# Float32 weights and tokens multiplied directly in the projections, their halves kept for the dense expert part

## The chip, the cores and the metric

The kernel runs on one core of one Trainium2 chip. The metric is the device time of one execution in microseconds (us); lower is better. In the profile the engines are PE (TensorE matmuls), PEld (TensorE's weight loads), DVE (VectorE), ACT (ScalarE), POOL (GpSimd) and SP (the queue that issues most transfers). L188 is line 188 of the kernel before.

## What is computed

Two transformer layers over 512 latent and 256 context tokens of width 1024, all in float32. Cut to what matters here:

```python
for i in range(2):
    xl = rmsnorm(hl, norm1_g[i]) * (1 + ml[1]) + ml[0]      # ml: 6 vectors from the conditioning
    xc = rmsnorm(hc, norm1_g[i]) * (1 + mc[1]) + mc[0]
    if i == 0:  # mLSTM heads and differential attention on xl @ w_in and xc @ w_in
        yl, yc = even_mixer(...)                            # each ends in concat(heads) @ w_out
    else:       # sliding-window attention, latent tokens alone
        yl = odd_mixer(...)
    hl = hl + ml[2] * yl                                    # and hc alike in layer 0
    x = rmsnorm(hl, norm2_g[i]) * (1 + ml[4]) + ml[3]
    hl = hl + ml[5] * peer(x)                               # and hc alike in layer 0
out = rmsnorm(hl, final_g)

def peer(x):   # 16384 experts of one neuron each
    q = (x @ w_q).reshape(n, 8, 2, 128)
    s = einsum('nhpd,hpkd->nhpk', q, keys)                  # scores of 2 x 128 keys per head
    # the 16 best keys of both sets, the 16 best sums of them: 128 experts a token
    gate = softmax(best sums)
    w = gate * gelu(x . u[expert])
    return sum of w * v[expert]
```

## The kernel before, in words

**Halves.** A float32 operand is split in two tiles of TensorE's rounded type float32r: the high half is the value rounded, the low half is the rest. A product of two such operands is three products of halves, high by high, high by low and low by high; a sum over 1024 rows is 8 steps of 128, so 24 matmuls of one pass each. The function `weight` (L178) loads a weight block of 512 KB, makes the high half `whi` on ACT (L185) and the low half `wlo` (L188) on DVE or POOL, in turn by the settings `WL1`, `WL2` and, in the latent mixer of layer 0, on POOL alone. `xpose` (L376) transposes a block of 128 tokens and splits it into `xth` (ACT, L383) and `xtl` (DVE, L384). `split` (L817) does the same for the mixer's output, which comes back from DRAM through a tile `yr` (L824, L825).

**Who uses them.** `projT` (L199) makes [128 outputs, T tokens] with T of 256, 384 or 512; `projN` (L208) makes [128 tokens, 256 outputs]. All projections of both mixers, both output projections and the routing's queries go through one of them. There are 195 weight blocks: 49 for the context tokens of layer 0, 67 for its latent tokens, 79 in layer 1; among them are the 18 and 27 expert blocks of the run-ahead products.

**The expert layer.** Each layer routes (`route`, L877: `scores` L858, then `select` L918), builds dense gates for 384 latent tokens (`gate_build`, L1044) and then runs over 128 groups of 128 experts (`peer`, L1323). For a group the first product `dense_u` (L1105) gives `dA`, a gelu and the gate give `dw`, and the second product (L1161) adds up in `dacc`. The first products of groups 0 to 17 (layer 0) or 0 to 26 (layer 1) run ahead, during routing and gate building. The other groups split their expert rows in `halves` (L1095) with a pool of buffers of their own.

**Gathered rows.** The context tokens and the last latent block fetch the rows of their experts one for each token by an indirect transfer that POOL issues (`gather`, L991, `uv` L998); DVE multiplies (`junkv`, L1011) or adds up (`pacc`, L1024) each row. Layer 0 has 768 such steps: 350 are issued at a low priority ahead of its dense part, 64 are left to the mixer of layer 1.

**Order.** Every engine runs its instructions in a fixed order, which the framework draws up when the program is built, by priorities and by a timeline that it simulates. [...]

**Stretches of time.** In the profiled execution: to 250 us the modulation and the context mixer of layer 0; to 420 the context tokens' routing; to 960 the latent mixer and its output projection; to 1510 routing and gate building; to 2520 the dense part; to 2955 the mixer of layer 1; to 3100 the routing's scores; to 3405 the selection and gates; then the dense part of layer 1.

The splitting of weights is this:

```python
hi = self.pw.tile(shape, F32R, name="whi", tag="whi", bufs=2)
lo = self.pw.tile(shape, F32R, name="wlo", tag="wlo", bufs=2)
nc.scalar.copy(hi, raw)
self.wcnt += 1
eng = nc.vector if self.wlo == 0 or self.wcnt % self.wlo == 0 else nc.gpsimd
eng.tensor_tensor(lo, raw, hi.bitcast(F32), op=OP.subtract)
```

## Time and profile before

| | before |
|---|---|
| three runs | 4350.32, 4350.83, 4351.87 us; median 4350.83 |
| the profiled execution's span, first to last instruction | 4350.6 us; no other time of that execution is recorded |
| busy: PE, PEld | 3739.3 us (86%), 3297.7 us (76%) |
| busy: DVE, ACT, POOL | 3715.8 us (85%), 1603.3 us (37%), 2683.4 us (62%) |
| DMA | 1093.10 MB in 16 engines, mean 251 GB/s |
| chain that ended last | PE 40%, DVE 25%, issue 15%, DMA 11%, POOL 7%, ACT 2% |

Busy times of an engine are unions over its instructions; matmuls are pipelined, so a matmul's time in a row is longer than the distance to the next one's start. The chain is followed back from the last instruction, at each step to what released it or to the instruction before it on its engine.

### The profile page before, as it was taken

The numbers are of one execution on the slowest core, as the hardware profiler recorded it, in microseconds if no ns is written. First come the engines' busy times: TensorE is split into PE (matmuls) and PEld (weight loads), VectorE is DVE, ScalarE is ACT, GpSimd is POOL, SyncE is SP. The second block draws the span as 40 slices with busy tenths as digits, with TensorE's granted clock in tenths as the row PEclk, the third lists the DMA queues.
The fourth block names the chain that finished last, engine by engine and source line by source line (L and its number), as shares of the span: only waits on it lengthen the run. The fifth ranks groups of instructions, "written<-read, shape, count | busy, mean of one in ns | idle before, by whom it ended". The sixth has DMA issues, their size and how long they took to land.

```text
span 4350.6 us, 58785 instructions
## 1 busy us (share of the span) xinstructions
PE 3739.3 (86%) x20576; PEld 3297.7 (76%) x20576; DVE 3715.8 (85%) x6089; ACT 1603.3 (37%) x2676; POOL 2683.4 (62%) x1886
## 2 busy tenths in 40 slices
PE   7977666756687699999999968899886999999999
PEld 5776654445567689988889857787875899999987
DVE  6479989979999998898989989747999887777788
ACT  4433433412115533333333325443245433333333
POOL 3146777656656677777878667112577676666664
PEclk9998888878798999999999989999989999999999
DMA  5554888788742499999899988423234987887878
GB/s 192 187 185 158 276 284 280 263 308 317 241 135 109 184 337 336 332 320 327 318 331 335 341 301 290 160 84 125 94 126 168 321 309 272 285 287 269 288 264 313
DMA packets 382487, 1093.10 MB, mean 251 GB/s; under 512 B 32671, under 2 KB 134375, under 8 KB 376046
## 3 DMA queue, kind: packets, MB, share of 16 engines
q0 software_dynamic: 147456, 536.94, 34.8%
q1 hardware_dynamic: 224942, 491.58, 32.9%
q10 hardware_dynamic: 9792, 60.82, 3.4%
q8 instruction: 162, 2.65, 0.2%
q14 instruction: 135, 1.11, 0.1%
HBM read 1020.96 MB, written 68.26 MB: 250 GB/s over the span
## 4 chain that ended last, share of the span: by engine, by line
PE 40%; DVE 25%; issue 15%; DMA 11%; POOL 7%; ACT 2%; SPq 0%; POOLq 0%; DVEq 0%; ACTq 0%
PE dacc L1161 17%; PE dA L1112 14%; POOL uv L998 4%; DVE ghot L1084 4%; DMA uv<-in_pr_u_dram,ix 3%; DMA draw<-in_uT_dram 3%; DVE junkv L1011 3%; DMA uv<-in_pr_v_dram,ix 2%; PE ops L214 1%; DVE wlo L188 1%; DVE pacc L1024 1%; PE pqps L204 1%; DVE sel L916 1%; DVE gup L1070 1%; DVE sel L913 1%
## 5 line engine op out<-in xcount | busy, mean ns | idle before, releaser
L1161 PE MATMUL dacc<-dhi,dw 128*128 128x512 f32 x3072 | 989.1, 392 | 3.4 <-ACT dw L1154 1.8
L998 POOL DMA_INDIRECT uv<-in_pr_v_dram,ix x512 | 685.6, 1339 | 405.0 <-DVE pacc L1024 297.6
L998 POOL DMA_INDIRECT uv<-in_pr_u_dram,ix x512 | 685.2, 1338 | 373.6 <-DVE pa L1011 204.3
L1011 DVE CUSTOM_DVE_ANT_0 junkv<-uv,x 128x1024 bf16<-128x1024 f32 x512 | 734.7, 1435 | 39.5 <-DMA uv<-in_pr_u_dram,ix 35.5
L1024 DVE SCALAR_TENSOR_TENSOR pacc<-uv,pw,pacc 128x1024 f32<-128x1024 f32 x508 | 705.1, 1388 | 26.9 <-DMA uv<-in_pr_v_dram,ix 23.0
L1161 PEld LDWEIGHTS dacc<-dhi,dw 128*128 128x128 f32 x3072 | 579.9, 189 | 120.7 <-ACT dw L1154 2.1
L1101 ACT CAST dhi<-draw 128x1024 fp32r<-128x1024 f32 x467 | 489.2, 1050 | 463.6 <-DMA draw<-in_uT_dram 165.9
L1161 PE MATMUL dacc<-dlo,dw 128*128 128x512 f32 x1536 | 604.4, 394 | 11.1 <-DVE dlo L1102 11.0
L1102 POOL TENSOR_TENSOR dlo<-draw,dhi 128x1024 fp32r<-128x1024 f32 x210 | 545.5, 2598 | 95.6 <-ACT dhi L1101 91.9
L188 POOL TENSOR_TENSOR wlo<-wraw,whi 128x1024 fp32r<-128x1024 f32 x111 | 280.0, 2523 | 426.0 <-ACT whi L185 282.1
L1151 DVE TENSOR_TENSOR dz<-dz,dG 128x384 f32<-128x384 f32 x256 | 402.4, 1585 | 89.9 <-ACT dz L1121 88.5
L1154 ACT CAST dw<-dz 128x384 fp32r<-128x384 f32 x256 | 131.4, 513 | 690.8 <-PE dacc L1161 669.8
L1102 DVE TENSOR_TENSOR dlo<-draw,dhi 128x1024 fp32r<-128x1024 f32 x257 | 336.1, 1308 | 27.3 <-ACT dhi L1101 18.1
L185 ACT CAST whi<-wraw 128x1024 fp32r<-128x1024 f32 x195 | 204.3, 1049 | 416.6 <-PE pqps L204 101.5
L1112 PE MATMUL dA<-xth,dhi 128*128 128x384 f32 x1688 | 334.8, 340 | 10.1 <-ACT dhi L1101 6.9
L1161 PEld LDWEIGHTS dacc<-dlo,dw 128*128 128x128 f32 x1536 | 289.8, 189 | 70.1 <-DVE dlo L1102 13.3
L1112 PE MATMUL dA<-xtl,dhi 128*128 128x384 f32 x1688 | 327.4, 335 | 0.0
L1112 PEld LDWEIGHTS dA<-xth,dhi 128*128 128x128 f32 x1688 | 305.1, 189 | 28.5 <-ACT dhi L1101 7.8
L1112 PE MATMUL dA<-xth,dlo 128*128 128x384 f32 x1688 | 326.7, 334 | 0.0
L1090 PE MATMUL gps<-ghot 128*128 128x128 f32 x1536 | 231.8, 307 | 104.5 <-DVE ghot L1084 80.2
L1090 PEld LDWEIGHTS gps<-ghot 128*128 128x128 f32 x1536 | 211.2, 216 | 126.3 <-issue 84.4
L1112 PEld LDWEIGHTS dA<-xtl,dhi 128*128 128x128 f32 x1688 | 296.7, 188 | 0.0
(379 smaller groups left out, 6836.6 us busy)
## 6 DMA issues: line engine op xcount, KB each, us to landing
draw<-in_pr_v_dram SPq DMA_DIRECT2D x256, 512.0 KB
draw<-in_uT_dram SPq DMA_DIRECT2D x211, 512.0 KB
wraw<-in_wb_dram SPq DMA_DIRECT2D x150, 512.0 KB
gd<-gch ACTq DMA_DIRECT2D x48, 1024.0 KB
dG<-gd SPq DMA_DIRECT2D x30, 1536.0 KB
wraw<-in_mod_t_dram SPq DMA_DIRECT2D x48, 512.0 KB
wraw<-in_uT_dram SPq DMA_DIRECT2D x45, 512.0 KB
wraw<-in_mod_w_dram SPq DMA_DIRECT2D x32, 512.0 KB
```

The lines of the kernel that those rows point to most:

```text
L185: nc.scalar.copy(hi, raw)
L188: eng.tensor_tensor(lo, raw, hi.bitcast(F32), op=OP.subtract)
L998: nc.gpsimd.indirect_dma_start(out=t, out_offset=None, in_=a[table], in_offset=bass.IndirectOffsetOnAxis(ap=ix[:, c:c + 1], axis=0))
L1011: nc.vector.tensor_tensor_reduce(out=junk, in0=u, in1=x, op0=OP.mult, op1=OP.add, scale=1.0, scalar=0.0, accum_out=A[:, c:c + 1])
L1024: nc.vector.scalar_tensor_tensor(acc, v, W[:, c:c + 1], acc, op0=OP.mult, op1=OP.add)
L1084: eng.tensor_tensor(h.rearrange("p t (a b) -> p t a b", b=16), up[:, e, t0:t0 + 4, :].unsqueeze(3).broadcast_to([128, 4, 8, 16]), low[:, e ...
L1090: nc.tensor.matmul(ps[:, t0 - 8 * q + t, :], hot[0][:, t, :], hot[1][:, t, :], start=True, stop=True)
L1101: nc.scalar.copy(hi, raw)
L1102: eng.tensor_tensor(lo, raw, hi.bitcast(F32), op=OP.subtract)
L1112: nc.tensor.matmul(A, u[ui][:, k, :], xt[xi][:, k, 0:ND], start=(i == 0), stop=(i == 23))
L1151: nc.vector.tensor_tensor(z3, z3, self.G[:, :, j % JG, :], op=OP.mult)
L1161: self.nc.tensor.matmul(acc[b][:, h, :], w[wi][:, 128 * b:128 * b + 128], v[vi][:, 512 * h:512 * h + 512], start=(j == 0 and i == 0), stop ...
```

## The change

`weight` returns the loaded float32 tile itself, with 5 buffers in place of 3 raw, 2 high and 2 low. `projT` and `projN` issue 8 float32 matmuls in place of 24 of halves. `xpose` copies the transposed tokens once, into one float32 tile. The mixer's output (`mixed`, before `split`) is loaded straight into that tile. The run-ahead products in `dense_u` take the float32 operands. Ahead of the dense part, `peer` splits the 384 tokens into `xh` (8 ACT copies and 8 DVE subtractions of 128x384); the dense part itself keeps its halves. The second buffer of the dense gates takes the place of the token tile. The loads of the first modulation use the new tiles. Changed lines, without those where a comment alone is removed and without the ones that follow from a name:

```diff
     def weight(self, src, shape):
-        nc = self.nc
-        raw = self.pw.tile(shape, F32, name="wraw", tag="wraw", bufs=3)
-        nc.sync.dma_start(raw, src)
-        hi = self.pw.tile(shape, F32R, name="whi", tag="whi", bufs=2)
-        lo = self.pw.tile(shape, F32R, name="wlo", tag="wlo", bufs=2)
-        nc.scalar.copy(hi, raw)
-        self.wcnt += 1
-        eng = nc.vector if self.wlo == 0 or self.wcnt % self.wlo == 0 else nc.gpsimd
-        eng.tensor_tensor(lo, raw, hi.bitcast(F32), op=OP.subtract)
-        return hi, lo
+        raw = self.pw.tile(shape, F32, name="wraw", tag="wraw", bufs=5)
+        self.nc.sync.dma_start(raw, src)
+        return raw
     def projT(self, ps, w, x, T, c0=0):
-        i = 0
-        for wi, xi in ((0, 0), (0, 1), (1, 0)):
-            for k in range(8):
-                self.nc.tensor.matmul(ps, w[wi][:, k, :], x[xi][:, k, c0:c0 + T],
-                                      start=(i == 0), stop=(i == 23))
-                i += 1
+        for k in range(8):
+            self.nc.tensor.matmul(ps, w[:, k, :], x[:, k, c0:c0 + T], start=(k == 0), stop=(k == 7))
     def projN(self, ps, w2, x, b):
...
+        for k in range(8):
+            self.nc.tensor.matmul(ps, x[:, k, 128 * b:128 * b + 128], w2[k // 4][:, k % 4, :],
+                                  start=(k == 0), stop=(k == 7))
     def mod_first(self):
...
-                if n < 8:
+                if n < 7:
                     if n % 4 == 0:
-                        four = self.xt.tile([128, 4, D], F32, name="fraw", tag="xt" + "hl"[n // 4])
+                        four = self.xt.tile([128, 4 - n // 4, D], F32, name="fraw", tag=("xt", "xhh")[n // 4])
                     raw = four[:, n % 4, :]
                 else:
-                    pool, tag, bufs = (self.pg, "uv", 5) if n < 13 else (self.pw, "wraw", 3)
+                    pool, tag, bufs = (self.pg, "uv", 5) if n < 12 else (self.pw, "wraw", 5)
     def xpose(self, x, xt, b):
...
-        hi = xt[0][:, :, 128 * b:128 * b + 128]
-        nc.scalar.copy(hi, p)
-        nc.vector.tensor_tensor(xt[1][:, :, 128 * b:128 * b + 128], p, hi.bitcast(F32), op=OP.subtract)
+        nc.scalar.copy(xt[:, :, 128 * b:128 * b + 128], p)
     def xt_tiles(self, T):
-        return tuple(self.px.tile([128, 8, T], F32R, name="xt" + x, tag="xt" + x) for x in "hl")
+        return self.px.tile([128, 8, T], F32, name="xt", tag="xt")
-    def split(self, l, bb, T):
+    def mixed(self, l, bb, T):
...
-            y = self.wk.tile([128, 2, T], F32, name="yr", tag="xn", bufs=2)
-            nc.sync.dma_start(y, self.yd[l, 128 * k:128 * k + 256, 128 * bb:128 * bb + T]
+            nc.sync.dma_start(xt[:, k:k + 2, :], self.yd[l, 128 * k:128 * k + 256, 128 * bb:128 * bb + T]
                               .rearrange("(k p) t -> p k t", p=128))
-            nc.scalar.copy(xt[0][:, k:k + 2, :], y)
-            nc.vector.tensor_tensor(xt[1][:, k:k + 2, :], y, xt[0][:, k:k + 2, :].bitcast(F32), op=OP.subtract)
     def dense_u(self, j, u, A, xt):
...
+        if j < self.upre:
+            self.projT(A, u, xt, ND)
+        else:
+            i = 0
+            for ui, xi in ((0, 0), (0, 1), (1, 0)):
...
     def load_gates(self, j, blocks):
...
-            self.G = self.dn.tile([128, ND // 16, JG, 16], F32, name="dG", tag="dG%d" % (j // JG % 2), bufs=1)
+            pool, tag = ((self.dn, "dG"), (self.xt, "xt"))[j // JG % 2]
+            self.G = pool.tile([128, ND // 16, JG, 16], F32, name="dG", tag=tag, bufs=1)
     def peer(self, l, xt, bb, gat, rows, done, late, put):
...
             gat += [(bb + b, LAT, sel[b]) for b in range(nd, nb)]
+            xh = [self.xt.tile([128, 8, ND], F32R, name="xh" + x, tag="xh" + x) for x in "hl"]
+            for k in range(8):
+                nc.scalar.copy(xh[0][:, k, :], xt[:, k, 0:ND])
+                nc.vector.tensor_tensor(xh[1][:, k, :], xt[:, k, 0:ND], xh[0][:, k, :].bitcast(F32), op=OP.subtract)
+            xt = xh
```

## Rows read from the trace of the kernel before

**Rows 1.** Windows by stretch: engines' busy us (instructions), granted clock, DMA share, GB/s

```profile
core 0: us, PE busy (x) PEld busy (x) DVE busy (x) ACT busy (x) POOL busy (x), PEclk, DMA share, GB/s
0.00:250.00 250.00, 208.95 (x1441) 162.93 (x1442) 130.75 (x249) 111.51 (x288) 63.48 (x59) 0.94 0.55 192
250.00:960.00 710.00, 482.97 (x2677) 405.48 (x2677) 629.57 (x1201) 245.14 (x611) 478.44 (x371) 0.83 0.74 251
960.00:1510.00 550.00, 393.06 (x2197) 343.38 (x2195) 531.93 (x1400) 165.35 (x169) 347.07 (x290) 0.86 0.56 200
1510.00:2520.00 1010.00, 991.22 (x4917) 892.27 (x4917) 923.02 (x899) 362.97 (x486) 767.85 (x455) 0.99 0.93 329
2520.00:2955.00 435.00, 361.44 (x2661) 319.80 (x2660) 320.45 (x381) 190.20 (x466) 169.23 (x157) 0.94 0.57 201
2955.00:3100.00 145.00, 133.12 (x668) 114.17 (x667) 126.65 (x646) 41.73 (x55) 44.42 (x39) 0.95 0.33 115
3100.00:3405.00 305.00, 233.26 (x1372) 217.68 (x1372) 286.22 (x557) 144.77 (x139) 210.82 (x169) 0.90 0.41 150
```

**Rows 2.** The chain that ended last, 250 to 960 and 960 to 1510, shares by line

```profile
by line: issue 18.7%; DMA uv<-in_pr_u_dram,ix 11.0%; DMA uv<-in_pr_v_dram,ix 6.4%; DVE pacc L1024 5.3%; POOL uv L998 4.6%; DVE junkv L1011 4.1%; DMA yr<-yd 2.8%; PE dao L797 2.5%; PE vps L214 2.1%; DMA mr<-modd 2.1%; PE ops L214 1.9%; DVE w
...
by line: issue 20.5%; DVE ghot L1084 14.0%; DVE junkv L1011 8.5%; DMA uv<-in_pr_u_dram,ix 5.2%; DVE gup L1070 4.6%; DVE sel L916 4.1%; DVE wlo L188 3.8%; DVE sel L913 3.8%; DVE glow L1070 3.5%; DVE sel L912 3.0%; DVE s L914 2.9%; DVE sel L9
```

**Rows 3.** Windows of line L188 alone (low halves of weights), by stretch

```profile
core 0: us, DVE busy (x) POOL busy (x), PEclk, DMA share, GB/s
0.00:250.00 250.00, 23.54 (x17) 43.58 (x18) 0.94 0.55 192
250.00:960.00 710.00, 14.25 (x9) 85.38 (x34) 0.83 0.74 251
960.00:1510.00 550.00, 32.10 (x19) 48.30 (x19) 0.86 0.56 200
2520.00:2955.00 435.00, 24.83 (x18) 46.00 (x18) 0.94 0.57 201
2955.00:3100.00 145.00, 14.60 (x10) 27.84 (x11) 0.95 0.33 115
3100.00:3405.00 305.00, 18.09 (x11) 28.93 (x11) 0.90 0.41 150
```

**Rows 4.** Low halves of tokens, from L384's own view: min/median/max ns

```profile
L384 DVE TENSOR_TENSOR xtl<-xps,xth x26: 1198/1220/1226, 47.9 to 2967.2; 128x1024 fp32r<-128x1024 f32 x26
```

**Rows 5.** Timelines of DVE and POOL near 1050 us: start us, us

```profile
1047.28 1.20 DVE L1011 CUSTOM_DVE_ANT_0 junkv<-uv,x 128x1024 bf16<-128x1024 f32 x1
...
1049.34 3.89 DVE L1011 CUSTOM_DVE_ANT_0 junkv<-uv,x 128x1024 bf16<-128x1024 f32 x1
...
1049.72 2.42 POOL L188 TENSOR_TENSOR wlo<-wraw,whi 128x1024 fp32r<-128x1024 f32 x1
```

**Rows 6.** Row products on DVE, 250 to 960, then 960 to 1510: count | busy us, mean ns

```profile
L1011 DVE CUSTOM_DVE_ANT_0 junkv<-uv,x 128x1024 bf16<-128x1024 f32 x129 | 181.7, 1409 | 27.8 <-DMA uv<-in_pr_u_dram,ix 25.9
...
L1011 DVE CUSTOM_DVE_ANT_0 junkv<-uv,x 128x1024 bf16<-128x1024 f32 x93 | 130.9, 1407 | 7.9 <-DMA uv<-in_pr_u_dram,ix 7.5
```

**Rows 7.** Timelines of POOL and DVE in layer 1's scores

```profile
2988.74 2.39 POOL L188 TENSOR_TENSOR wlo<-wraw,whi 128x1024 fp32r<-128x1024 f32 x1 [8.45 <-PE pqps L204]
...
2989.38 0.29 DVE L912 MAX8 sel<-pss 128x8 f32<-128x128 f32 x1
```

**Rows 8.** Chain pieces of 24 matmuls of halves, 512 and 384 columns: start us, us

```profile
3000.83 5.46 PE pqps L204 x24
...
3405.46 4.19 PE dA L1112 x24
```

**Rows 9.** Timeline of PE: halves at 256 columns, then float32 at 512 and 256

```profile
2930.25 0.63 PE L214 MATMUL ops<-whi,xth 128*128 128x256 f32 x4
2930.72 0.63 PE L214 MATMUL ops<-wlo,xth 128*128 128x256 f32 x4
...
867.61 0.60 PE L772 MATMUL das<-kdc,qpd 128*128 128x256 f32 x2
868.04 1.02 PE L772 MATMUL das<-ktd,qpd 128*128 128x512 f32 x2
868.90 0.60 PE L772 MATMUL das<-kdc,qpd 128*128 128x256 f32 x2
```

**Rows 10.** The page's row of the high halves of weights

```profile
L185 ACT CAST whi<-wraw 128x1024 fp32r<-128x1024 f32 x195 | 204.3, 1049 | 416.6 <-PE pqps L204 101.5
```

More of the change, by code (lines that the diff above doesn't have):

```diff
@@ L114, in __init__ @@
         self.wk = None
-        self.wcnt, self.wlo, self.ghot = 0, WL1, 0
+        self.ghot = 0
         nc = self.nc
@@ L199, in projT @@
     def projT(self, ps, w, x, T, c0=0):
-        i = 0
-        for wi, xi in ((0, 0), (0, 1), (1, 0)):
-            for k in range(8):
-                self.nc.tensor.matmul(ps, w[wi][:, k, :], x[xi][:, k, c0:c0 + T],
-                                      start=(i == 0), stop=(i == 23))
-                i += 1
-    def projN(self, ps, w2, x, b):
-        i = 0
-        for half in range(2):
-            for xi, wi in ((0, 0), (0, 1), (1, 0)):
-                for k in range(4):
-                    self.nc.tensor.matmul(
-                        ps, x[xi][:, 4 * half + k, 128 * b:128 * b + 128], w2[half][wi][:, k, :],
-                        start=(i == 0), stop=(i == 23))
-                    i += 1
+        for k in range(8):
+            self.nc.tensor.matmul(ps, w[:, k, :], x[:, k, c0:c0 + T], start=(k == 0), stop=(k == 7))
+    def projN(self, ps, w2, x, b):
+        for k in range(8):
+            self.nc.tensor.matmul(ps, x[:, k, 128 * b:128 * b + 128], w2[k // 4][:, k % 4, :],
+                                  start=(k == 0), stop=(k == 7))
     def mod_prep(self):
@@ L241, in mod @@
                 for h in range(2):
-                    raw = self.pw.tile([128, 8, 128], F32, name="wraw", tag="wraw", bufs=3)
+                    raw = self.pw.tile([128, 8, 128], F32, name="wraw", tag="wraw", bufs=5)
                     nc.sync.dma_start(raw, a["mod_t"][l, m, 2 * q + h])
@@ L321, in mod_rows @@
             for k in range(8):
-                raw = self.pw.tile([128, D], F32, name="wraw", tag="wraw", bufs=3)
+                raw = self.pw.tile([128, D], F32, name="wraw", tag="wraw", bufs=5)
                 nc.sync.dma_start(raw, a["mod_w"][l][128 * k:128 * k + 128, m * D:m * D + D])
@@ L698, in head_out @@
         else:
-            hi, lo = (t[:, k, tok] for t in self.yx)
-            nc.scalar.copy(hi, pt)
-            nc.vector.tensor_tensor(lo, pt, hi.bitcast(F32), op=OP.subtract)
+            nc.scalar.copy(self.yx[:, k, tok], pt)
     def rope(self, ps, T, outs, c0=0, scale=None):
@@ L830, in out_proj @@
         nc = self.nc
-        xt = xt or self.split(l, hb, 128 * nb)
+        xt = self.mixed(l, hb, 128 * nb) if xt is None else xt
         m2 = self.modrow(l, s, 2)
@@ L1108, in dense_u @@
         nc = self.nc
-        i = 0
-        for ui, xi in ((0, 0), (0, 1), (1, 0)):
-            for k in range(8):
-                nc.tensor.matmul(A, u[ui][:, k, :], xt[xi][:, k, 0:ND], start=(i == 0), stop=(i == 23))
-                i += 1
+        if j < self.upre:
[4 more added lines that the diff above has]
+                for k in range(8):
+                    nc.tensor.matmul(A, u[ui][:, k, :], xt[xi][:, k, 0:ND], start=(i == 0), stop=(i == 23))
+                    i += 1
         if j % (self.ahead + 1) <= self.upre:
@@ L1345, in peer @@
             gat += [(bb + b, LAT, sel[b]) for b in range(nd, nb)]
+            xh = [self.xt.tile([128, 8, ND], F32R, name="xh" + x, tag="xh" + x) for x in "hl"]
+            for k in range(8):
+                nc.scalar.copy(xh[0][:, k, :], xt[:, k, 0:ND])
+                nc.vector.tensor_tensor(xh[1][:, k, :], xt[:, k, 0:ND], xh[0][:, k, :].bitcast(F32), op=OP.subtract)
+            xt = xh
             left, done = 256 * len(gat) - done - late, 0
@@ L1402, in run @@
                     self.mod(0, M1)
-                    self.yx = [self.px.tile([128, 8, 256], F32R, name="yx" + x) for x in "hl"]
+                    self.yx = self.px.tile([128, 8, 256], F32, name="yx")
                     self.even(CTX, xt, 2, 0)
@@ L1408, in run @@
                                            lambda: self.mod(0, F5[0]), self.yx)
-                    self.px, self.wlo = px, WL2
+                    self.px = px
                     with self.phase("rt"):
@@ L1420, in run @@
                         next(rows)
-                self.px, self.wlo = px, 1 << 30
+                self.px = px
                 self.even(LAT, xt, 4, 2)
-                self.wlo = 2
             with self.phase("op"):
```

1 line of the change is left out of this document (removed).

## The prediction

> **What bounds the kernel now.** I read the windows by stretch first, because TensorE's 86% over the whole span hides stretches with different limits. Both dense parts are TensorE's: between 1510 and 2520 us it is busy 991 of 1010 us [rows 1], and neither the change's matmuls nor its splits of weights lie there. What can move is the other 2395 us. There the reader should put PE and DVE side by side. From 250 to 1510 us DVE is busy 629.57 + 531.93 = 1161.5 of 1260 us (92%; 97% from 960 on) and PE 876.0 (70%). From 3100 to 3405 it is 94% against 76%. From 2955 to 3100, the scores of layer 1, PE leads with 92%, and in the first stretch and the mixer of layer 1 it leads too, with 84% and 83% against 52% and 74% [rows 1].
>
> The chain of waits, read second, says how far a busy engine sets the end. From 960 to 1510 the named pieces are mostly DVE's: one-hot rows, row products, searches. From 250 to 960 DVE has a smaller part; 11.0% and 6.4% are waits for gathered rows on their way, and 18.7% is issue [rows 2]. So DVE time removed after 960 should come back nearly in full, before 960 in part.
>
> **What the change takes off.** Off ACT go 195 high halves of 1.05 us, 204 us in all [rows 10]; ACT is busy for 29% to 47% of the stretches, so I cost this at nothing [rows 1]. If ACT were on the path, the same 204 us would be the price. Off DVE and POOL go the low halves: 127 us on DVE and 280 us on POOL over the six stretches [rows 3]. Off DVE also go the tokens' low halves at 1.22 us [rows 4], 26 from transposes and 4 in the load of the mixer's output, which has the same 1024 columns.
>
> POOL's 280 us matter for a second reason. A row product on DVE takes 1.20 us, but 3.89 us when a POOL low half of 2.42 us runs inside it: DVE lost 2.69 us [rows 5]. The 222 row products between 250 and 1510 average 1.41 us, so they alone lost 222 x 0.21 = 46 us [rows 6] beside 133.7 us of POOL low halves [rows 3]. Other two-operand instructions must lose too, so the stall that goes lies between 46 and 134 us in that stretch. I take 0.6 of POOL's time, 80 us, above the lower end because the 46 covers one kind of instruction. Not every DVE instruction loses: a search for the maximum, which reads one operand, takes 0.29 us while a POOL low half is running [rows 7]. In layer 1's scores, where DVE has little else, I therefore count no stall. [...]
>
> **What it adds.** A group of 24 matmuls of halves takes 5.46 us at 512 columns and 4.19 at 384 [rows 8]; at 256 columns 4 take 0.47 us (2930.25 to 2930.72), so 24 take 2.82 [rows 9]. A float32 matmul stands in the trace as two records. One record at 512 columns takes (868.90 - 868.04)/2 = 0.43 us, at 256 columns (868.04 - 867.61)/2 = 0.215 [rows 9]. Sixteen records are then 6.88 us at 512, 3.44 at 256, and between them about 5.16 at 384, which no row shows directly. A group grows by 1.42, 0.97 and 0.62 us. The code has 45 groups at 512 columns, 47 at 384 and 131 at 256: 64 + 46 + 81 = 191 us more PE work. [...]
>
> **The sum by stretch.** PE's extra counts by a quarter where DVE leads, because PE then has 24 to 32% idle to take it, by a half where PE leads among waits on other engines, and in full where matmuls run back to back.
>
> - To 250: 33 groups at 256, +20.5 us, half: +10. Removed DVE work is off the path there; I take 4 us of it for shorter starts. Net +6.
> - 250 to 960: off DVE 14.3 us of weights [rows 3], ten token or output halves (12.2 us) and 0.6 x 85.4 = 51 us of stalls, 78 in all. Half of it, since the chain holds row transfers and issue: -39. PE: 56 groups at 256 and 13 at 512, +53 us, a quarter: +13. Net -26.
> - 960 to 1510: off DVE 32.1 + 4.9 + 0.6 x 48.3 = 66 us. The new split of tokens puts back 8 instructions of at most 0.6 us (half of [rows 4]), 5 us; 61 remain. Three quarters: -46. PE: 16 groups at 512 and 18 at 384, +40 us, a quarter: +10. Net -36.
> - 2520 to 2955: 42 groups at 256 and 2 at 384, +28 us, half: +14. DVE sheds 24.8 us, some ten token halves and 28 us of stalls, but it doesn't lead: -6. Net +8.
> - 2955 to 3100: the 16 score groups run back to back, and 5.46 us each [rows 8] become 6.88: +23. Four token halves ahead of them go: -3. Net +20.
> - 3100 to 3405: off DVE 18.1 + 0.6 x 28.9 - 5 = 30 us, three quarters: -23. PE: 27 groups at 384, +26 us, a quarter: +7. Net -16.
> - Dense parts: 0. They keep their buffers and halves, and the split of tokens is counted above. The second gate buffer waits for the token tile's last reader, which is that split, some groups before group 8 needs the buffer; if that cover were gone, one load of 1.5 MB would stand open per layer, 6 us at the mean of 251 GB/s.
>
> Together 6 - 26 - 36 + 8 + 20 - 16 = -44 us. From the profiled span of 4350.6 us this is 4307 us; the span lies 0.2 us from the runs' median of 4350.83, so nothing is added.
>
> The 2 raw buffers more replace the 2 prepared blocks of before, so loads run as far ahead: I cost this at nothing, because the DMA share outside the dense parts is 0.33 to 0.74 [rows 1] (uncovered, a 512 KB block would cost 2.1 us at the mean of 251 GB/s). Gathered steps keep their number; since POOL issues them in order behind its low halves, they can start up to 2.4 us earlier behind each of 53.
>
> **The rivals.**
>
> *TensorE takes over (slower).* The added passes land on the path in proportion to PE's busy share: 0.84 x 20.5 + 0.68 x 53 + 0.71 x 40 + 0.83 x 28 + 23 + 0.76 x 26 = 17 + 36 + 28 + 23 + 23 + 20 = 147 us. Against this stand the same gains as in my sum, 4 + 39 + 46 + 6 + 3 + 23 = 121. The result is +26, 4377, and a few us more where a single projection heads a chain of waits: up to 4390. It decides once more than 63% (121/191) of the added work lies on the path; my sum has 10 + 13 + 10 + 14 + 23 + 7 = 77 us there (40%). For it: 83 to 92% busy in three of the six stretches. Against: from 250 to 1510 PE is idle 384 us.
>
> *DVE's time comes back in full.* All 78 + 61 + 30 us in place of 39 + 46 + 23: another -61, 4246; with stalls at their upper end, POOL's whole 133.7 us in place of 80, up to 50 more, 4196. For it: 97% and 94% busy. Against: the waits for rows and issue in the chain.
>
> *No change.* Between 250 and 960 DVE only waits longer for gathered rows (17.4% of the chain already), and the 39 us don't come: 4346. For it: a DMA share of 0.74 there. Against: DVE is busy for 89% of that stretch, waiting little.
>
> **How the numbers follow.** A measurement of this kernel can tell about 0.2% (9 us) from no change. Chances: my sum, 4260 to 4340, 0.48; full return, 0.17; no change, 0.11; TensorE takes over, 0.24. Faster is 0.48 + 0.17 = 0.65, same 0.11, slower 0.24. The range of 8 in 10 goes from 4205, near the lower end of full return, to 4390, the end of the slower case. The likeliest time is 4307.
>
> **What would show it.** PE busy should rise by about 190 us and DVE fall by 200 to 300 (127 of weights, 37 of tokens, the stalls). Row products between 250 and the dense part should average near 1.2 us in place of 1.41. Score groups in layer 1 should repeat 1.4 us later each. A run-ahead group at 384 columns should take 5.1 to 5.2 us. The first dense part should begin some 55 us sooner, the mixer of layer 1 should be longer by 8, and from its end to the second dense part nothing should change by more than 10. I am wrong if the row products stay above 1.35 us, for then something else on POOL stalls them; if PE in 250 to 1510 passes 80% busy with DVE waiting for projections; or if the built order places the gathered rows elsewhere, so that mixer and routing shift against one another.

## The result and the profile after

The changed kernel takes 4249.89 us (median of four runs, 4238.75 to 4256.38) against 4351.35 (4350.32 to 4356.29) for the kernel before: the ratio is 0.9761, 95% interval 0.9745 to 0.9777. 101 us were gained where 44 were forecast. The profiled execution took 4256.38 us with a span of 4254.5; it lies 96 us below the profiled span of before.

The page of the changed kernel gives the engines' busy time and the chain by engine:

```profile
PE 3836.0 (90%) x18792; PEld 3131.2 (74%) x18792; DVE 3429.5 (81%) x5975; ACT 1416.7 (33%) x2493; POOL 2376.5 (56%) x1775
...
PE 49%; DVE 18%; DMA 13%; issue 11%; POOL 7%; ACT 2%; SPq 0%; POOLq 0%; ACTq 0%; DVEq 0%
```

DVE fell by 286 us and POOL by 307; PE rose by 97 only, not by 190. The chain went from 25% DVE to 18% and from 40% PE to 49%.

To compare stretches I use events in place of fixed times, since everything shifts. First starts in the two traces, us:

| event | before | after | shift | gained in the stretch that ends here |
|---|---|---|---|---|
| context queries (`pqps`) | 254.5 | 260.9 | +6.4 | +6.4 |
| latent queries, layer 0 | 1024.4 | 1006.0 | -18.4 | -24.8 |
| `dacc`, layer 0 | 1525.1 | 1442.4 | -82.7 | -64.3 |
| queries of layer 1 | 2968.6 | 2871.5 | -97.1 | -14.4 |
| end of the last query, layer 1 | 3072.9 | 2996.4 | -76.5 | +20.6 |
| `dacc`, layer 1 | 3393.8 | 3296.3 | -97.5 | -21.0 |

The forecast's steps were +6, -26, -36, +8, +20, -16. Four are within 5 us. The two that miss are the scores, selection and gates of layer 0 (28 us more gained) and the stretch with the mixer of layer 1 (22 more); the border at 960 lies in the output projection, so the first of these is a little blurred.

Windows of the kernel before, from the latent mixer to its output projection, then the scores of layer 0, then those of the changed kernel: the same two, the selection, and the scores of layer 1 [rows 1 have the columns].

```profile
345.60:907.70 562.10, 373.20 (x1862) 305.03 (x1862) 506.11 (x796) 206.53 (x550) 410.02 (x322) 0.81 0.77 258
1024.40:1200.50 176.10, 127.75 (x480) 101.31 (x480) 172.00 (x594) 24.51 (x31) 105.39 (x97) 0.79 0.77 262
```

```profile
349.80:922.90 573.10, 400.43 (x1591) 285.65 (x1591) 487.90 (x758) 180.28 (x522) 384.24 (x313) 0.82 0.81 284
...
1006.00:1138.10 132.10, 125.56 (x354) 61.66 (x355) 124.11 (x568) 8.49 (x16) 61.56 (x72) 0.96 0.75 271
1138.10:1222.70 84.60, 74.17 (x415) 48.73 (x413) 83.69 (x402) 5.63 (x15) 36.54 (x46) 0.97 0.46 150
...
2871.50:2996.40 124.90, 124.90 (x369) 62.30 (x370) 87.28 (x558) 9.43 (x18) 16.74 (x27) 0.98 0.27 93
```

The latent mixer became 11 us longer; the scores of layer 0 became 44 us shorter. In the scores DVE was busy for 172.00 of 176.1 us and is now for 124.11 of 132.1: the bound has become PE, 95% busy. In the scores of layer 1 PE has no idle time left.

Row products on DVE (count | busy us, mean ns), in the kernel before ahead of the latent queries (345.6 to 1024.4 us), from there to the end of selection (none follows until the dense part), and over 250 to 1510; then the same of the changed kernel (349.8 to 1006; to the gates' end; 250 to 1427):

```profile
L1011 DVE CUSTOM_DVE_ANT_0 junkv<-uv,x 128x1024 bf16<-128x1024 f32 x157 | 219.3, 1397 | 32.4 <-DMA uv<-in_pr_u_dram,ix 30.3
...
L1011 DVE CUSTOM_DVE_ANT_0 junkv<-uv,x 128x1024 bf16<-128x1024 f32 x66 | 94.5, 1432 | 5.6 <-DMA uv<-in_pr_u_dram,ix 5.5
...
L1011 DVE CUSTOM_DVE_ANT_0 junkv<-uv,x 128x1024 bf16<-128x1024 f32 x222 | 312.6, 1408 | 35.7 <-DMA uv<-in_pr_u_dram,ix 33.5
```

```profile
L987 DVE CUSTOM_DVE_ANT_0 junkv<-uv,x 128x1024 bf16<-128x1024 f32 x177 | 223.2, 1261 | 57.1 <-DMA uv<-in_pr_u_dram,ix 55.0
...
L987 DVE CUSTOM_DVE_ANT_0 junkv<-uv,x 128x1024 bf16<-128x1024 f32 x46 | 55.6, 1208 | 7.0 <-DMA uv<-in_pr_u_dram,ix 6.8
...
L987 DVE CUSTOM_DVE_ANT_0 junkv<-uv,x 128x1024 bf16<-128x1024 f32 x222 | 277.6, 1250 | 64.0 <-DMA uv<-in_pr_u_dram,ix 61.8
```

The 222 products are the same, at 1.25 us in place of 1.41. But 20 of them went from behind the latent queries to ahead of them: 177 in place of 157, and 46 in place of 66. So time that DVE gained in the latent mixer shows up later, as rows that no longer take DVE's time in the scores.

The chain of the changed kernel has the new groups at their full size, 16 records at 512 columns and at 384:

```profile
2888.62 6.87 PE pqps L194 x16
...
3121.64 5.16 PE dA L194 x16
```

These are the 6.88 and 5.16 us of the forecast. The price of a group was right at this clock (0.98 granted in the scores of layer 1, 0.95 in its gates).

### The profile page after: what moved, and what is told of

It reads as the page before. It is cut to its first block, busy times and chain, and to the rows that moved or that the text cites. A ratio compares the mean times of both kernels' runs of the same rounds, so it can differ in the third digit from the quotient of the medians.

```text
span 4254.5 us, 54646 instructions
## 1 busy us (share of the span) xinstructions
PE 3836.0 (90%) x18792; PEld 3131.2 (74%) x18792; DVE 3429.5 (81%) x5975; ACT 1416.7 (33%) x2493; POOL 2376.5 (56%) x1775
## 4 chain that ended last, share of the span: by engine, by line
PE 49%; DVE 18%; DMA 13%; issue 11%; POOL 7%; ACT 2%; SPq 0%; POOLq 0%; ACTq 0%; DVEq 0%
PE dacc L1141 17%; PE dA L1091 13%; POOL uv L974 5%; DMA uv<-in_pr_v_dram,ix 4%; DMA uv<-in_pr_u_dram,ix 3%; DMA draw<-in_uT_dram 3%; PE ops L199 3%; PE dA L194 3%; PE pqps L194 2%; DVE junkv L987 2%; PE gps L1066 2%; DVE ghot L1060 2%; POOL dlo L1078 1%; PE oo L1298 1%; DVE sel L941 1%
## 5 line engine op out<-in xcount | busy, mean ns | idle before, releaser
L987 DVE CUSTOM_DVE_ANT_0 junkv<-uv,x 128x1024 bf16<-128x1024 f32 x512 | 700.1, 1367 | 69.2 <-DMA uv<-in_pr_u_dram,ix 65.1
L1077 ACT CAST dhi<-draw 128x1024 fp32r<-128x1024 f32 x467 | 489.5, 1050 | 494.4 <-DMA draw<-in_uT_dram 162.5
L1091 PE MATMUL dA<-xhh,dhi 128*128 128x384 f32 x1688 | 334.5, 340 | 11.3 <-ACT dhi L1077 6.9
L1091 PE MATMUL dA<-xhl,dhi 128*128 128x384 f32 x1688 | 327.6, 335 | 0.0
L1091 PE MATMUL dA<-xhh,dlo 128*128 128x384 f32 x1688 | 326.7, 334 | 0.3 <-POOL dlo L1078 0.3
L1091 PEld LDWEIGHTS dA<-xhh,dhi 128*128 128x128 f32 x1688 | 305.0, 189 | 29.4 <-ACT dhi L1077 7.3
L194 PE MATMUL pqps<-xt,wraw 128*128 128x512 f32 (+1 forms) x768 | 289.9, 532 | 8.8 <-DMA wraw<-in_wb_dram 6.2
L1091 PEld LDWEIGHTS dA<-xhl,dhi 128*128 128x128 f32 x1688 | 296.9, 188 | 0.1
L1091 PEld LDWEIGHTS dA<-xhh,dlo 128*128 128x128 f32 x1688 | 295.6, 188 | 0.7 <-POOL dlo L1078 0.6
L1135 DVE TENSOR_TENSOR dw<-dz,dw 128x384 fp32r<-128x384 f32 x256 | 170.4, 666 | 150.5 <-ACT dw L1134 150.5
L1066 PE MATMUL gps<-ghot 128*128 128x128 f32 x1536 | 219.2, 301 | 75.8 <-DVE ghot L1060 59.7
```

The costliest lines, as they stand in the source:

```text
L194: self.nc.tensor.matmul(ps, w[:, k, :], x[:, k, c0:c0 + T], start=(k == 0), stop=(k == 7))
L987: nc.vector.tensor_tensor_reduce(out=junk, in0=u, in1=x, op0=OP.mult, op1=OP.add, scale=1.0, scalar=0.0, accum_out=A[:, c:c + 1])
L1066: nc.tensor.matmul(ps[:, t0 - 8 * q + t, :], hot[0][:, t, :], hot[1][:, t, :], start=True, stop=True)
L1091: nc.tensor.matmul(A, u[ui][:, k, :], xt[xi][:, k, 0:ND], start=(i == 0), stop=(i == 23))
L1135: i = nc.vector.tensor_tensor(wl, z, wh.bitcast(F32), op=OP.subtract)
```

## The experiments

Each was timed in three rounds beside the kernel before, whose medians there were 4348.5 to 4352.6. Medians:

| label | kernel | us |
|---|---|---|
| | changed | 4249.89 |
| e8, e7 | changed, 4 or 3 raw buffers | 4261.41, 4258.69 |
| e2 | changed, 4 raw buffers, POOL's subtractions of weights back | 4335.37 |
| e3 | changed, 4 raw buffers, DVE's back | 4293.79 |
| e9, e17 | changed, 4 or 3 raw buffers, both back | 4385.21, 4388.71 |
| e18 | e17, tokens' halves and staged load back | 4406.22 |
| e11 | changed, 4 raw buffers, tokens' halves back | 4270.32 |
| e10 | changed, 3 raw buffers, weights copied by ACT | 4264.17 |
| e5 | changed, staged load | 4250.15 |
| e4 | changed, 6 of 8 matmuls a group | 4143.38 |
| e14 | before, 30 matmuls a group | 4418.88 |
| e1 | before, low halves all on DVE | 4297.14 |
| e15 | before, routing on DVE | 4300.63 |
| e16 | e1, routing on DVE | 4247.62 |
| e6, e12 | changed, one-hot rows on DVE; gates' product too | 4230.48, 4237.72 |
| e13 | e12, selection's products on DVE too | 4186.45 |

Runs of one kernel spread by 5 to 28 us, so a difference of less than about 10 us between two medians is not held to be one.

**Subtractions put back, POOL's alone, DVE's alone, neither.** The products stay float32; `raw - raw` goes to a tile that nothing reads, in the turn of before. POOL's alone:

```diff
     def weight(self, src, shape):
...
-        raw = self.pw.tile(shape, F32, name="wraw", tag="wraw", bufs=5)
+        raw = self.pw.tile(shape, F32, name="wraw", tag="wraw", bufs=4)
         self.nc.sync.dma_start(raw, src)
+        self.wcnt += 1
+        if self.wlo == 0 or self.wcnt % self.wlo == 0:
+            pass
+        else:
+            lo = self.pw.tile(shape, F32R, name="wlo", tag="wlo", bufs=1)
+            self.nc.gpsimd.tensor_tensor(lo, raw, raw, op=OP.subtract)
         return raw
```

> The changed kernel, with POOL's 111 low-half subtractions put back in the turn of before; their results are used by nothing, the products stay float32, and the raw tiles have 4 buffers in place of 5 to make room. Theory A (the gain is mainly POOL's: its low halves stalled DVE's two-operand instructions and stood before the gathers): with stalls of 0.6 of POOL's time, back in full in the three stretches where DVE leads (51 + 29 + 17 us), about 4250 + 97 = 4347 us, and the row products between 250 us and the first dense part average 1.4 us again. By the shares of the prediction (half, three quarters, three quarters) 26 + 22 + 13 = 61: 4311. Theory B (the gain is DVE's own instructions that went): under 4265, whatever the row products take.

> The changed kernel, with DVE's 84 low-half subtractions of weights put back in the turn of before; their results are used by nothing, and the raw tiles have 4 buffers in place of 5. No POOL subtraction stands beside them, so each should take the 1.22 us of a token's low half. Theory B (DVE's own work): the 39 in the three stretches where DVE leads come back in full, 48 us, and some of the others: 4298 to 4310. By the shares of the prediction (half of 11, three quarters of 23 and of 13) 33: 4283. Theory A (POOL's stalls are the gain): under 4270, since DVE now has slack before it leads again.

> The changed kernel with 4 raw buffers in place of 5 and nothing else: what the two runs with subtractions put back are to be held against. The prediction costed the depth at nothing: 4250, within 9 us. The rival is that loads which run further ahead are a part of the gain that the sum left out: 4265 or more, with longer waits of PE for weights at the start of projections.

Against the 4261 with 4 buffers POOL's 111 subtractions cost 74 us, more than by the prediction's shares (61), less than in full (97). DVE's 84 cost 32, as the shares say. Neither theory holds alone: B wanted under 4265 with POOL's back, A under 4270 with DVE's. The timelines of DVE and of POOL in the run with POOL's show how:

```profile
1042.92 1.23 DVE L993 CUSTOM_DVE_ANT_0 junkv<-uv,x 128x1024 bf16<-128x1024 f32 x1
...
1044.20 2.78 DVE L993 CUSTOM_DVE_ANT_0 junkv<-uv,x 128x1024 bf16<-128x1024 f32 x1
...
1047.02 1.22 DVE L993 CUSTOM_DVE_ANT_0 junkv<-uv,x 128x1024 bf16<-128x1024 f32 x1
...
1048.29 2.79 DVE L993 CUSTOM_DVE_ANT_0 junkv<-uv,x 128x1024 bf16<-128x1024 f32 x1
```

```profile
1043.70 2.20 POOL L186 TENSOR_TENSOR wlo<-wraw 128x1024 fp32r<-128x1024 f32 x1
...
1047.83 2.16 POOL L186 TENSOR_TENSOR wlo<-wraw 128x1024 fp32r<-128x1024 f32 x1
```

Each subtraction that starts at 1043.70 and 1047.83 ends at 1045.90 and 1049.99; the row product that starts behind it (1044.20, 1048.29) ends 1.08 us and 1.09 us after that end, as though it had only then begun. Where POOL starts first, as in these two pairs, the row product takes 2.78 and 2.79 us. The row products just before, at 1042.92 and 1047.02, started 0.78 and 0.81 us ahead of POOL; they took their usual 1.2 us, and POOL's took 2.20 and 2.16 us where most of POOL's that meet no row product take 1.90.

**Low halves on DVE, in the kernel before** (`WL1, WL2 = 1, 1`, and the latent mixer's too):

> The kernel before with all low halves of weights on DVE: no POOL subtraction of a weight is left outside the dense parts, and DVE has 111 more of 1.22 us, 135 us in all, 78 of them where DVE leads. Theory A with stalls in full: 4351 - 97 + 78 = 4332. By the prediction's shares 4351 - 61 + 48 = 4338. Theory B (stalls cost little): 4351 + 60 = 4410.

It gained 51 us on the 4348.54 timed beside it, though DVE has 111 instructions more; that is more than either form of theory A had expected. Row products fell to 1.27 us. POOL's halves were a loss already in the kernel before.

**Both put back.**

> The changed kernel with all 195 unused subtractions put back, on POOL and DVE in the turn of before, 4 raw buffers. If POOL's and DVE's shares add (74 and 32 over the 4261 of the run with 4 buffers): 4367. If they draw on one slack: 4340. What is left of the difference to the kernel before is then float32 on TensorE, the high halves and the tokens' halves together: the prediction's sum puts these at +77 and about -17, 4411; a time near 4350 means that the added passes cost about as little as the tokens' halves gave.

124 over the run with 4 buffers, 18 more than 74 + 32. The two wrote one scratch tile; with a tile each and 3 buffers:

> The changed kernel with 3 raw buffers in place of 5: what the next two are held against. With 4 buffers it was 4261 (11 us more). If depth has its price on each step, 4272; if only the block that is loaded ahead counted, 4261.

> The changed kernel with 3 raw buffers and all 195 unused subtractions, DVE's and POOL's results in a tile of their own each; in the run before they shared one tile, so that DVE had to wait for POOL's. If the 18 us by which both together cost more than each alone (124 against 74 + 32) came from that shared tile: 106 over the run with 3 buffers alone. If from DVE and POOL stalling one another: 124 again.

4389 against 4259 is 130, so the shared tile wasn't it: with both put back the row products average 1.40 us, as before the change, against 1.36 with POOL's alone. DVE's 84 now cost some 56 us on top of POOL's 74, where alone they cost 32. That each makes the other dearer was measured twice (18 and 24 us); by which waits was not looked into. The buffers beyond 3 or 4 are worth 9 to 11 us, near what the spread lets one tell; the prediction had them at nothing.

**Tokens, copies, staged load.** Each by itself, from the changed kernel:

```diff
+        hi = self.pw.tile(shape, F32, name="whi", tag="whi", bufs=2)     # e10, in weight
+        self.nc.scalar.copy(hi, raw)
+        return hi
...
+        lo = self.pw.tile([128, 8, 128], F32R, name="xlo", tag="xlo", bufs=1)   # e11, in xpose
+        nc.vector.tensor_tensor(lo, p, xt[:, :, 128 * b:128 * b + 128], op=OP.subtract)
...
+            y = self.wk.tile([128, 2, T], F32, name="yr", tag="xn", bufs=2)     # e5, in mixed
+            nc.sync.dma_start(y, self.yd[l, 128 * k:128 * k + 256, 128 * bb:128 * bb + T]
...
+            nc.scalar.copy(xt[:, k:k + 2, :], y)
```

> The changed kernel with each weight block copied by ACT to a second float32 tile, from which the products read it, as the high half was made before: 3 raw buffers and 2 copies, 195 copies of about 1.05 us, 204 us on ACT. The prediction costed these at nothing: 4250, within 9, or 4261 with the run of 4 buffers as a measure of loads that run less far ahead. Theory D (what the sum left out is the step between a weight's arrival and its product, and ACT's time): 58 us of the measured gain are in no run yet (101 us gained, 81 us of it lost again to TensorE by the run with six of eight matmuls, so 182 in all, of which the subtractions of weights are 124); with all of the 58 here 4308, with half 4279.

> The changed kernel with the 26 low halves of transposed tokens put back on DVE, their results unused, 4 raw buffers: 26 x 1.22 = 32 us. By the prediction's shares about 19 us over the 4261 with 4 buffers: 4280. Theory D (the 58 us that are left lie with the weights' copies): under 4275. Theory E (they lie with the tokens, which stand at the head of every projection): 4300 or more.

> The changed kernel with the mixer's output loaded through two staging tiles and copied by ACT, as before, without a low half. The prediction costed the direct load at its low halves alone: 4250 within 9. Theory C (the wait for these copies ahead of both output projections is a part of the gain that the sum left out: in the kernel before PE waited 31 us for them): 4270 to 4280, with the output projection of the latent mixer begun later.

None costs much: 5 us for 195 copies of 1.05 us on ACT against the 3-buffer run, 9 for the tokens against the 4-buffer run, nothing for the staged load by the medians (in its profile the first `dacc` comes 7 us later, at 1449.7, and a dense part that is 13 us shorter makes up for it). Theories C, D and E fall as larger causes. The staged load did delay PE at the output projection, and the first query came 19 us later (1024.7 in place of 1006.0); the gates of layer 0 then began at 1226.9 in place of 1222.7, as DVE, not PE, leads to the end of that stretch (83.69 of 84.60 us in the changed kernel). PE's row of that run and of the changed kernel, 880 to 1030 us:

```profile
L199 PE MATMUL ops<-wraw,xt 128*128 128x256 f32 x256 | 62.1, 405 | 31.7 <-ACT xt L803 28.5 <-DVE ot L822 3.2
```

```profile
L199 PE MATMUL ops<-wraw,xt 128*128 128x256 f32 x232 | 53.8, 396 | 16.2 <-DMA xt<-yd 11.9 <-DVE ot L820 4.3
```

All of it together, on top of both subtractions:

> The same, with the 26 low halves of transposed tokens and the staged load of the mixer's output (its ACT copy and its low half on DVE) put back as well, their results unused. Everything that DVE and POOL did before is then done again, and float32 on TensorE, ACT's copies of weights and the waits for halves are what is left of the change. If the tokens' halves cost the 9 us of the run that had them alone: 9 over the run before it. If they cost more where DVE has no slack, which would close the 17 us that no run has found: 25 to 35 over it, near the 4419 of the kernel before with 30 matmuls a group.

17.5 us over the run before it, twice the 9 that the tokens cost by themselves, less than the 25 expected for closing the gap. What remains against the kernel before (4406 - 4352 = 54 us) is float32 on TensorE and the new split of the tokens, less ACT's copies and the waits for halves.

**TensorE's added work by itself.** From the changed kernel with `range(6)` for `range(8)` in `projT` and 6 of 8 steps in `projN`, which leaves a quarter of each sum out, and from the kernel before with 6 more matmuls, low half by low half:

```diff
+        for k in range(6):
+            self.nc.tensor.matmul(ps, w[1][:, k, :], x[1][:, k, c0:c0 + T], start=False, stop=(i == 29))
+            i += 1
```

> The changed kernel with 6 of the 8 matmuls in each group of a projection and of a run-ahead product; a quarter of each sum is left out. A group at 512 columns takes 12 records of 0.43 us, 5.16 us, near the 5.46 of halves before, so this takes off TensorE about what the change put on, 45 x 1.72 + 47 x 1.29 + 131 x 0.86 = 251 us against the 191 added. By the prediction's share of 40% on the path 251 x 0.4 = 100: 4250 - 100 = 4150. If the added passes are hidden but in the scores of layer 1: 4250 - 16 x 1.72 = 4222. If TensorE became the bound of the projections everywhere, 63% or more, 4092 or less.

> The kernel before, halves and all, with 30 matmuls in place of 24 in each group of a projection and of a run-ahead product: the 6 more are low half by low half. A group takes 5.46 x 30 / 24 = 6.83 us at 512 columns (float32: 6.88), 5.24 at 384 and 3.53 at 256; 62 + 49 + 93 = 204 us are added, near the 191 of the change, and nothing else moves. By the prediction's share of 40%: 4351 + 82 = 4433. By what the other runs leave (the run with all subtractions put back lies 35 us above before and still lacks the tokens' halves, 9, and the weights' copies, up to 14): 4351 + 58 = 4409 or less. If DVE's lead covers nearly all of it in the kernel before: 4351 + 23 for the scores of layer 1 and little more, under 4385.

The first gained 107 of 251 us (43%), near the forecast's 40%; the second cost 67 of 204 (33%). For the 191 of the change that is 81 by the kernel whose DVE is relieved and 63 by the one whose DVE is loaded; the 54 of the run above is near the second. Busy windows of the queries alone in layer 0, then layer 1, of the kernel before, and of the changed one, show where 16 of the rest stayed:

```profile
1024.40:1200.50 176.10, 108.93 (x384) 84.16 (x384) 8.20 (x14) 0.79 0.77 262
2968.60:3073.00 104.40, 92.33 (x384) 72.20 (x384) 8.78 (x15) 0.98 0.28 94
```

```profile
1006.00:1138.10 132.10, 115.08 (x256) 49.08 (x256) 8.07 (x14) 0.96 0.75 271
2871.50:2996.40 124.90, 114.68 (x256) 48.34 (x256) 8.76 (x15) 0.98 0.27 93
```

(The columns are PE, PEld, ACT, granted clock, DMA share, GB/s.) At equal clocks, in layer 1, the queries grew by 22.4 us, as forecast. In layer 0 they grew by 6.2, because halves ran there at a mean granted clock of 0.79, with PE busy for 73% of the stretch, and float32 at 0.96, with PE busy for 95%. The same 384 matmuls of halves took 108.93 us at 0.79 and 92.33 at 0.98. The 0.79 is a mean over the stretch: from 1007 to 1030 us the granted clock was 0.50, from 1031 to 1081 it was 1.00.

**Where POOL still does two-operand work.** `GENG = "v"` puts all one-hot rows on DVE; the next runs also move the gates' product and the selection's products:

```diff
-GENG = "vpvpvvvp"
+GENG = "v"
...
-            nc.gpsimd.tensor_tensor(ge, ge, diff.unsqueeze(2).broadcast_to([128, 4, 16, 16]), op=OP.mult)
+            nc.vector.tensor_tensor(ge, ge, diff.unsqueeze(2).broadcast_to([128, 4, 16, 16]), op=OP.mult)
...
-                nc.gpsimd.tensor_tensor(low[:, 1], low[:, 1],
+                nc.vector.tensor_tensor(low[:, 1], low[:, 1],
```

> The changed kernel with all one-hot rows of the gate building on DVE (before: 120 of 192 a layer there, 72 on POOL). In the first gate building DVE's 120 average 1.07 us beside POOL's, their median is 0.69. Theory A carried further (POOL instructions with two operands slow DVE's): 192 x 0.69 = 132 us in place of 122, no stalls in the others, and PE no longer waits for POOL's rows: 4250 - 10 to - 30. The rival: DVE leads in the gate building and any added instruction there is paid: 144 x 0.69 = 99 us less 92 of stalls, 4255 or more.

> The run with all one-hot rows on DVE (4230), and the gates' multiplication into the low rows (22 of 1.0 us a layer on POOL) on DVE too. Theory A, that POOL's two-operand work costs DVE more than its own doing: 22 x 0.5 us on DVE a layer against stalls of the same size, 4220 to 4230. The rival, that DVE's added time is paid in full: 4252.

> The same, and the multiplications of the selection (128x1024, 2.5 us on POOL) on DVE too, 1.23 us each: no two-operand instruction of POOL is then left in the routing. Selection is where DVE leads with 84 of 85 us. Theory A: each took DVE about 0.5 us of stall and a wait of its own for POOL's 2.5 us, so within 10 us of the run before it, either way. The rival: DVE's time is paid in full, 32 x 1.23 = 39 us more, 4260 or above.

The one-hot rows gained 19 us, as theory A said. The gates' product alone moved nothing that can be told. With the selection's products on DVE as well, 4186.45 us: 63 under the changed kernel, 51 under the run before it, where theory A had expected no change and the rival a loss. It is the best of all (0.9624 of the kernel before, 0.9608 to 0.964). One-hot rows on DVE in the changed kernel, and in this one, first layer:

```profile
L1060 DVE TENSOR_TENSOR ghot<-gup,glow 128x512 f32<-128x512 f32 x120 | 122.1, 1069 | 14.9 <-PE gps L1066 14.9
```

```profile
L1060 DVE TENSOR_TENSOR ghot<-gup,glow 128x512 f32<-128x512 f32 x192 | 119.4, 677 | 3.8 <-PE gps L1066 3.6
...
L944 DVE TENSOR_TENSOR sel<-sel 128x1024 f32<-128x1024 f32 x16 | 19.4, 1211 | 0.0
```

DVE makes 192 in less time than it made 120 beside POOL's 72. Of the selection's 40 products the 16 for the latent tokens of layer 0 are shown; they take 1.21 us each on DVE, and the step no longer crosses to POOL and back. Which of the two, POOL's relief or the crossing that is saved, gives the 51 us isn't shown.

**Does the gain need float32 products?** The same relief of POOL on the kernel before, and on the kernel with all low halves on DVE:

> The kernel before with the one-hot rows, the gates' multiplication and the selection's multiplications on DVE; the low halves of weights stay on POOL and DVE in turn. The changed kernel gained 64 us from the same edit (4250 to 4186). If that edit and the change work apart from one another: 4351 - 64 = 4287. If the low halves on POOL still stall DVE's added instructions as well: a third to a half of it, 4320 to 4330.

> The kernel before with halves everywhere, all low halves on DVE and the routing's two-operand instructions on DVE as well: POOL is relieved in the same way as in the best kernel so far (4186), but TensorE has its 24 matmuls of halves and DVE 195 low halves. If relieving POOL is nearly all that float32 products are worth: within 15 us of 4186. If the two edits add, 4297 - 64 = 4233: then float32 products are worth 47 us beyond POOL's relief.

The routing's edit gained 51 us by itself in the kernel before, and 63 on top of the change: together they don't give less than apart (165 against 101 + 51), but a little more, near what the spread lets one tell. Halves with POOL relieved take 4248 us, what the changed kernel takes; with float32 products and the same relief it is 4186. All low halves on DVE and the routing's edit add (4297 less 51 is 4246), and float32 products are worth 61 us beyond POOL's relief. The rival that POOL's relief is all of it falls.

## Why the direction was right and the size wrong

Differences between first starts in the traces, stretch by stretch as in the first table (us): the 6 extra matmuls (e14 less before), both subtractions (e17 less e7), tokens and staged load (e18 less e17), fewer buffers (e7 less changed). The stretch up to the queries of layer 1 is divided at the end of the last `dacc` of layer 0, in a dense part and a mixer.

| stretch ends with | matmuls | subtractions | tokens, load | buffers |
|---|---|---|---|---|
| context queries | 12.5 | 5.0 | 3.1 | -0.5 |
| latent queries | 35.3 | 42.3 | 24.0 | -9.7 |
| `dacc`, layer 0 | -18.3 | 46.1 | -9.4 | 8.2 |
| last `dacc`, layer 0 | 0.9 | 10.6 | -15.8 | -9.5 |
| queries of layer 1 | 24.1 | 7.0 | 13.8 | 13.2 |
| last query of layer 1 | 19.8 | 0.7 | -0.7 | 0.6 |
| `dacc`, layer 1 | -5.8 | 19.4 | -3.4 | -0.6 |

No edit changes what the dense part of layer 0 computes, yet it takes 986.6 to 1004.4 us in the 20 traces, in no order that follows the edits (in layer 1 it takes 946.4 to 947.8). Why isn't known. Windows of it and of the mixer behind it, in the kernel before, the changed one and e18 [rows 1 have the columns]:

```profile
1525.10:2528.60 1003.50, 988.45 (x4897) 888.04 (x4895) 919.38 (x895) 354.07 (x476) 766.08 (x457) 0.99 0.93 330
2528.60:2968.60 440.00, 359.07 (x2650) 317.91 (x2649) 325.30 (x385) 197.20 (x476) 165.66 (x153) 0.93 0.58 203
```

```profile
1442.40:2445.60 1003.20, 984.54 (x4897) 884.14 (x4895) 921.36 (x896) 353.55 (x476) 767.87 (x457) 1.00 0.93 330
2445.60:2871.50 425.90, 375.38 (x2298) 313.49 (x2297) 269.51 (x359) 164.21 (x446) 106.48 (x135) 0.96 0.57 206
```

```profile
1551.50:2540.00 988.50, 983.04 (x4898) 886.04 (x4896) 918.50 (x893) 354.31 (x476) 766.93 (x457) 1.00 0.95 334
2540.00:2999.90 459.90, 380.89 (x2297) 318.44 (x2296) 327.86 (x392) 164.96 (x446) 151.76 (x153) 0.93 0.56 194
```

The step that failed is the share of DVE's and POOL's removed work that comes back. The prediction had 121 us of it on the path (128 before the new split was taken off), and 77 of TensorE's added work against it; the runs have 148, and 54 to 63.

- **Subtractions of weights: right in kind, too small.** The prediction's shares give 33 + 46 + 27, about 105 us where DVE leads, and part of the 10 that it didn't divide (4 and 6). Measured: 130. Put back apart, POOL's 74 and DVE's 32 come to that 105; the rest is what each costs more beside the other, for which the sum had no term. From 250 us to the first dense part it is 88 for 79: up to the latent queries "half of it, since the chain holds row transfers and issue" was too low a share (42 for 33, and 9 row products of 173 were left for later besides), behind them three quarters held (46).
- **The mixer of layer 1: a miss of its own.** There the prediction had 6 us for everything that DVE and POOL shed ("it doesn't lead"). In e18, which does it all again with 3 buffers, the mixer takes 459.9 us, in the changed kernel 425.9: 34 us. An engine with 74% busy time was not free there. How the 34 divide isn't shown: both subtractions cost 7 there with 3 raw buffers, 19 with 4, and POOL's alone 21.
- **TensorE's added work: groups sized right, their share not one number.** 77 was forecast. With DVE loaded 63 were measured, or 54 by what e18 leaves; with DVE relieved it would be 81. From 250 us to the first `dacc` it cost 17.0 where 23 was forecast, in the gates of layer 1 it cost nothing (-5.8) where 7 was, and in the mixer 24 where 14 was. In e14 the longer latent mixer took in 14 more row products ahead of the latent queries (171 for 157), and in the scores of layer 0 the granted clock rose from 0.79 to 0.91. The scores of layer 1 took 20 us in both, of 23 forecast. The rival that TensorE takes over falls; 33% to 43% of the added work lay on the path, not 63%.
- **Tokens' halves and the staged load: 13 forecast, less 7 for the new split; 17.5 measured** with DVE loaded, 9 for the tokens alone with DVE relieved. No run takes the new split out.
- **High halves on ACT at nothing: right**, 5 us for 195 copies. **Buffers at nothing: short by about 9 us**, near what the spread lets one tell.
- **Dense parts: right.** From the first `dacc` to the last they take 1003.2 us against 1003.5 in layer 0, and 947.8 against 946.4 in layer 1.

By these runs the terms erred in the same direction: 130 + 17.5 + 9 - 54 = 102 us. The runs are steps of one chain, so that the sum closes is no proof of its terms; only the 54, which is what is left over, has another measurement beside it, the 63. The total came out near the rival of full return (4246), but that is luck and not its mechanism: neither DVE's nor POOL's time came back in full (88 us of the 126 of DVE's subtractions and estimated stalls from 250 to 1510). Luck is also in two of the stretches that agreed. Up to the latent queries the runs have 66 us for subtractions, tokens and load against 35 for TensorE's added work, where the forecast had 39 against 13; in the gates of layer 1 they have 16 and no cost, where it had 23 against 7.

Of the prediction's signs, the row products (1.25 us), the groups and DVE's fall came as said. PE's busy time rose by 97 us where 190 was said; 16 of the difference is the clock in the queries of layer 0, the rest wasn't divided. The first dense part began 83 us sooner where 55 was said, and the mixer of layer 1 became 14 us shorter where it was to be longer by 8. One of its signs of being wrong came true: the built order moved gathered rows, 20 from the routing to ahead of it.

What stays open: the 54 us are measured between two whole kernels. In the profiled executions these differ by 47.5 us (4398.1 and 4350.6), and the dense part of layer 0 is 15.0 us shorter in the one with everything put back; without that difference it would be 63, as the extra matmuls say, which may be chance, since the new split and the copies are in it too. In the mixer of layer 1 the run with everything put back lies 19.9 us above the kernel before, and the extra matmuls cost 24.1 there. ACT's copies cost about 2 us in that mixer against the 3-buffer run; the products' wait for low halves wasn't tried.

## What to carry to other kernels

Price a POOL instruction with two operands by what it costs DVE beside it, not by POOL's idle time: moving such work to a DVE that was already busy for 92% (the kernel before) or 87% (the changed one) of the time from 250 us to the first dense part made the kernel faster three times here (51, 51 and 63 us). Test a cost by putting it back unused into the new kernel, and put the parts back together as well as alone: apart they gave 106 us, together 124 to 130. Where gathered rows fill an engine's gaps, sum over the whole stretch up to the point where they must be done; time saved early can come back late (here as 20 row products fewer behind the latent queries). And before a stretch is compared, take out what no edit changed: a dense part varied by 18 us here.

## What the runs showed of the hardware that was not expected

- The products of the selection moved from POOL to DVE, which leads in that stretch with 83.69 of 84.60 us, and the time fell by 51 us from the run before. Little of it lies in that stretch: the latent selection of layer 0 took 83.3 us in the run before and takes 81.3. From the last context query to the first latent one, where the context tokens are selected and the latent mixer runs, it went from 681.7 to 655.7 us; the scores behind it became 8 us longer, the gates 13 and 11 us shorter. Windows of the kernel with routing on DVE: selection, then the gates of both layers.

```profile
1127.80:1209.10 81.30, 79.04 (x436) 52.68 (x435) 81.30 (x424) 6.11 (x16) 14.14 (x34) 1.00 0.51 163
1209.10:1404.70 195.60, 161.93 (x966) 131.49 (x966) 185.27 (x395) 112.01 (x88) 15.68 (x10) 0.97 0.45 167
3009.50:3226.60 217.10, 191.26 (x1051) 149.77 (x1049) 183.01 (x392) 116.26 (x100) 23.47 (x14) 0.95 0.49 176
```

POOL is busy for 15.68 of 195.60 us in the first gates, where it was for 135.88 of 219.70 in the changed kernel; nearly all of that went with the one-hot rows and the gates' product, since it was 21.60 of 208.40 in the run before.

- In the scores of layer 0 the granted clock was 0.79 in the kernel before, with PE busy for 73% of the stretch, and 0.96 in the changed one, with 95%; that paid for 16 of the 22 us that its queries would have grown by. Why the clock was higher isn't shown.

- Of a row product and a POOL low half that overlap, which one is slow went here with how far apart their start stamps lie, and the one with the earlier stamp isn't always the quick one. In the run with POOL's put back, 19 row products that overlap a low half have the earlier stamp. Where POOL's follows by 0.58 us or less (6 times) the row product took 3.1 to 4.3 us; where it follows by 0.64 us or more (13 times) the row product took 1.2 us, and POOL's 2.05 to 2.32 in place of 1.90. Over all seven kernels with low halves on POOL, and pairs of one and one, 46 of 48 row products were slow when POOL's began less than 0.6 us behind them, and 77 of 79 were not when it began later. The prediction's pair, 0.38 us apart, is of the first kind.

```profile
1110.36 3.56 DVE L993 CUSTOM_DVE_ANT_0 junkv<-uv,x 128x1024 bf16<-128x1024 f32 x1
...
1110.93 1.90 POOL L186 TENSOR_TENSOR wlo<-wraw 128x1024 fp32r<-128x1024 f32 x1
```
